# A two-layer trunk on one core: output pieces of the feed-forward stages dealt out in another order

## The chip, the core and the metric

The kernel runs on one core of a Trainium2 chip. A core has engines that run side by side, each with its own queue of instructions worked off in order: TensorE (PE in the profile: matmuls and transposes, with PEld for its weight loads), VectorE (DVE), ScalarE (ACT), GpSimd (POOL, here mostly a source of DMAs) and SyncE (SP, here only DMAs). They meet through semaphores. Matmuls write into PSUM, eight banks of 128 x 512 floats; everything else lives in SBUF. The metric is the device time of one execution in microseconds (us).

## The reference

The input is `x`, 256 tokens of 1024 floats. Two layers follow, each of three steps with a residual and a layer norm:

```
for i in range(2):
    x = LN(alpha * x + 0.5 * swiglu_ffn(x, ffn1_w_in[i], ffn1_w_out[i]))
    x = LN(alpha * x + mixer_i(x))          # 0: sparse attention, 1: state-space scan
    x = LN(alpha * x + 0.5 * swiglu_ffn(x, ffn2_w_in[i], ffn2_w_out[i]))

def swiglu_ffn(x, w_in, w_out):
    gate, up = jnp.split(x @ w_in, 2, axis=-1)      # 1024 -> 2 x 2816
    return (jax.nn.silu(gate) * up) @ w_out         # 2816 -> 1024
```

So there are four feed-forward stages (FFNs), and the change is in them. The mixers stay as they are, except that the scan's last projection ends in the same helper, `tail`.

## The kernel before

**Numbers in two parts.** Every matmul operand is split into a high part (ScalarE casts it, `wh` at L324 for weights, `hH` for activations) and a low remainder (VectorE subtracts, `wl` at L352, `hL`). A product is three matmuls per tile: high by high (L530), one low (L531) and the other low (L532); the helper is `mm3`.

**Weights.** All weights stream through in one long list of units of 128 x 1024 floats, 512 KB. SyncE loads a unit (`raw`, L243), ScalarE makes `wh`, VectorE makes `wl`; a ring of 10 slots holds the pairs. Some units are sums of two loaded ones: VectorE adds them (L291), or GpSimd starts a DMA that adds (L264). `W.pump` makes the next units at given points of the program, so the place of every cast and subtraction in ScalarE's and VectorE's queues is fixed when the program is written. So is everything else: there is no scheduler. Small steps (`later`) are queued by the program and emitted some `step()`s after they were asked for.

**A feed-forward stage.** The inner width 2816 is 22 blocks of 128. `ffn` makes them in three ways:

- *wide*: blocks 0 to 3 as two groups of two. In the first FFN both token halves run side by side; in the other three the first token half (t=0) of both groups comes first, then t=1.
- *seven(j)*: blocks j to j+3 by seven half-size products in place of eight. The products come in the order A11, Q1, piece, Q4, S2, piece, S3, A12, piece, A22, piece; each is 12 matmuls with two units of weights. Two PSUM banks `pmm` (X, Y) and one `ptr` (Z) hold them; ScalarE copies X and Y out (L935, L936, L942, L947), VectorE combines (L919 to L929), and `glu` (L771) does silu on ScalarE (L775) and the multiplication on VectorE (L780). Q1, Q4, S2 and S3 take sums of the activations (`xf`), made by `xT.sums` in eight parts; the others take `xT`.
- *one(j)*: a single block, R below, as two halves, gate and up. Each half is 8 matmuls of 512 columns (L679) and 8 of 256 (L681) into one bank; then ScalarE copies one side out (L887) and VectorE adds the other (L888), which frees the bank. Even blocks use the `pmm` banks, odd ones the `ptr` banks. `turn` (L761) also takes `ptr` banks in turn, for the transposes (L767) of finished activations; ScalarE (L768) and VectorE (L769) split them into `hH` and `hL`.

An *output piece* j multiplies finished activations of block j with 128 rows of the second weight: 12 matmuls into the four `acc` banks, one unit. It can be put anywhere after block j is finished. Pieces thus fill TensorE while other engines prepare the next product. The last six pieces of a stage go to `tail`, which orders them so that the first token half's layer norm can start early: all six pieces of one column half, then all six of the other.

`ffn_steps` deals out the blocks and pieces for all four FFNs alike: S4 with pieces 0, 1, 2, 3; S8 with 6, 7, 4, 5; S12 with 10, 11, 8, 9; S16 with 14, 15, 12, 13; R20; R21; and the tail with 16 to 21. So in all four FFNs the blocks made last (20, 21) are the last two of the tail's list, and the tail follows right behind R21.

Of the kernel before, what the change touches and what calls it, by code (L numbers as in the profile page):

```python
# [21 lines left out]
NJ = FF // 128  # L22
# [38 lines left out]


WIDE = 2
LAG = 6
SEVEN = (4, 8, 12, 16)
MOST = 2500


def ffn_steps():


    steps = []
    for j in SEVEN:
        steps.append(('S', j, [[j - 2], [j - 1], [j - 4], [j - 3]] if j > SEVEN[0] else [[0], [1], [2], [3]]))
    steps += [('R', j, []) for j in range(SEVEN[-1] + 4, NJ)]
    return steps


def ffn_units(ws, wi, wo, wide, lag):
    def colblk(c0):  # L80
        return wi[:, c0:c0 + 128]

    def ktile(blk):
        n = blk.shape[1]
        return blk.reshape(DK, 128, n).transpose(1, 0, 2)

    def out_unit(j):
        ws.append(wo[j * 128:(j + 1) * 128])

    for w in range(wide):  # L90
        j = 2 * w
        blk = np.concatenate([wi[:, j * 128:(j + 2) * 128], wi[:, FF + j * 128:FF + (j + 2) * 128]], axis=1)
        t = ktile(blk)
        for k in range(0, DK, 2):
            ws.append(t[:, k:k + 2].reshape(128, -1))
    def quarter(j, kh):

        blk = np.concatenate([wi[:, j * 128:(j + 2) * 128], wi[:, FF + j * 128:FF + (j + 2) * 128]], axis=1)
        t = ktile(blk)
        return [t[:, k:k + 2].reshape(128, -1) for k in (4 * kh, 4 * kh + 2)]  # L100

    for kind, j, outs in ffn_steps():
        if kind == 'S':
            outs = list(outs)

            def out():
                for o in outs.pop(0):
                    out_unit(o)
# [24 lines left out]


# [57 lines left out]

def all_units(v):
    ws = Plan()
    ffn_units(ws, v['ffn1_w_in'][0], v['ffn1_w_out'][0], WIDE, LAG)
    attn_units(ws, v['attn_w_in'][0], v['attn_w_uk'][0], v['attn_w_uv'][0], v['attn_w_out'][0])
    ffn_units(ws, v['ffn2_w_in'][0], v['ffn2_w_out'][0], WIDE, LAG)
    ffn_units(ws, v['ffn1_w_in'][1], v['ffn1_w_out'][1], WIDE, LAG)
    ssd_units(ws, v['ssm_w_in'][0], v['ssm_w_out'][0])
    ffn_units(ws, v['ffn2_w_in'][1], v['ffn2_w_out'][1], WIDE, LAG)  # L200
    return ws


# [205 lines left out]
def trunk_kernel(ctx: ExitStack, tc: tile.TileContext, widths, forms, x, ln_g, ln_b, wts, kvg, convp,  # L409
                 dt_bias, a_log, d_skip, norm_g, out):  # L410
    nc = tc.nc
# [14 lines left out]
    def f4(s):  # L426
        return wk.tile([128, 1024], F32, name=nm(s), tag="f4", bufs=12)
# [16 lines left out]
    def pmm():  # L444
        return psum.tile([128, 512], F32, name=nm("pmm"), tag="pmm", bufs=2)
# [244 lines left out]
    def tail(acc, c, gb, ks, u, lhs, first, last, hook=None, early=0, ff=False):  # L690

        n = len(ks)
        nxt = None
        m = 0 if last else n - 3
        order = [[(i, hf) for hf in range(2) for i in range(n)],
                 [(i, hf) for i in range(m) for hf in range(2)] + [(i, hf) for hf in range(2) for i in range(m, n)]]
        W.highs(8)
        W.lows()  # L700
        for t in range(2):
            for s, (i, hf) in enumerate(order[t]):
                if s == n and not t and hook:
                    hook()
                if s == n + FILL and t and not last:
                    nxt = XT(ff)
                    nxt.fill(0)
                H, L = W.get(u + i)
                if t and hf and last:
                    continue  # L710
                cs = slice(hf * 512, (hf + 1) * 512)
                mm3(acc[t][hf], *lhs(ks[i], t), H[:, cs], L[:, cs], first and i == 0, i == n - 1)
                if t and hf:
                    W.free(u + i)
                    if s < 2 * n - 2:
                        W.highs()
                        if s < n + FILL - early:
                            W.lows()
            rest = None
            if t and last:  # L720
                rest = pmm()[:, :256]
                for q, ps in enumerate((acc[t][1][:, :256], rest)):
                    ws = slice(512 + q * 256, 768 + q * 256)
                    for i, k in enumerate(ks):
                        H, L = W.get(u + i)
                        mm3(ps, *lhs(k, t), H[:, ws], L[:, ws], q == 1 and i == 0, i == n - 1)
            if t:
                W.lows(len(W.late) - 2)
            layernorm(t, acc[t], c, gb, last, rest, (lambda: W.lows(len(W.late) - 1)) if t and not last else None)
            if not t:  # L730
                W.highs(8)
                W.lows()
        return nxt

    def ffn(xT, u0, ln_i, first=False, last=False, ff=False):
# [3 lines left out]
        u = u0  # L739
# [31 lines left out]
        def glu(t, w, c, sil=None):  # L771


            g, h = (c[:, :256], c[:, 256:]) if sil is None else (sil, f1("h"))
            nc.scalar.activation(g, c[:, :256], AF.Silu)  # L775
            if sil is not None and w >= WIDE:
                nc.scalar.copy(h, c[:, 256:])

            def mul():
                nc.vector.tensor_mul(h, h if w >= WIDE else c[:, 256:], g)  # L780
# [10 lines left out]
        if first:  # L791
# [3 lines left out]
            for w in range(WIDE):  # L795
                ps = [ptr(), ptr()] if w else [pmm(), pmm()]
                for k in range(0, DK, 2):
                    for t in range(2):
                        if (w, k, t) == (0, 0, 1):
                            W.pump(1, now=True)  # L800
                        if (w, k) == (0, 2):
                            xT.fill(t, [1])
                            W.pump(1 + 2 * t, now=True)
                        if (w, k, t) == (0, 4, 1):
                            W.pump(3, now=True)
                        wide(t, w, ps[t], k, k + 2)
# [35 lines left out]
        acc = {}  # L842
# [60 lines left out]
        def seven(j, outs):  # L903


            outs = list(outs)
# [838 lines left out]
```

## Time and profile before

| what | value |
|---|---|
| time, median of 3 runs | 1027.97 us (1027.45 to 1029.94) |
| the profiled execution | 1026.81 us, of which the span of the trace is 1025.0 us |
| busy: PE, DVE, ACT, POOL | 1006.6, 907.9, 660.8, 121.4 us |
| HBM traffic | 193.48 MB read, 190 GB/s over the span |
| first FFN | 0 to 187.65 us |
| sparse attention | 187.65 to 291.14 us |
| second FFN | 291.14 to 469.73 us |
| third FFN | 469.73 to 648.10 us |
| state-space scan | 648.10 to 842.00 us |
| last FFN | 842.00 to 1025.00 us |

How to read it: a row of the timeline gives the start, the length, the engine, the line, what is written and read, and in square brackets how long the engine had stood idle and what released it. One matmul of 512 columns occupies some 0.39 us in these rows, but the next one starts 0.23 us after it; so starts, not lengths, are to be compared on PE. A group row gives the sum of busy time, the mean length in ns, and the idle time before the group with its releasers.

### The profile page before, as it was taken

The numbers are of one execution on the slowest core, as the hardware profiler recorded it, in microseconds if no ns is written. First come the engines' busy times: TensorE is split into PE (matmuls) and PEld (weight loads), VectorE is DVE, ScalarE is ACT, GpSimd is POOL, SyncE is SP. The second block draws the span as 40 slices with busy tenths as digits, with TensorE's granted clock in tenths as the row PEclk, the third lists the DMA queues.
The fourth block names the chain that finished last, engine by engine and source line by source line (L and its number), as shares of the span: only waits on it lengthen the run. The fifth ranks groups of instructions, "written<-read, shape, count | busy, mean of one in ns | idle before, by whom it ended". The sixth has DMA issues, their size and how long they took to land.

```text
span 1025.0 us, 14615 instructions
## 1 busy us (share of the span) xinstructions
PE 1006.6 (98%) x5279; PEld 848.2 (83%) x5279; DVE 907.9 (89%) x1264; ACT 660.8 (64%) x962; POOL 121.4 (12%) x179
## 2 busy tenths in 40 slices
PE   8999999999999999999999999999999999999996
PEld 7788888888787888888778888999899887888885
DVE  6899998789789999988999998788999978999985
ACT  6666776477656667764666775486876645777760
POOL 2101100100011011001101100151111110101101
PEclk9999999999999999999999999999999999999999
DMA  9899999352547899992789999358665654899861
GB/s 332 217 287 276 296 258 360 103 150 98 186 144 171 263 284 295 258 375 78 177 263 281 298 253 348 132 164 249 193 219 187 202 207 108 274 266 254 257 237 41
DMA packets 64664, 231.70 MB, mean 226 GB/s; under 512 B 7280, under 2 KB 7344, under 8 KB 64592
## 3 DMA queue, kind: packets, MB, share of 16 engines
q1 hardware_dynamic: 51264, 183.43, 49.2%
q0 software_dynamic: 13040, 46.82, 23.6%
q8 instruction: 41, 0.67, 0.3%
q10 hardware_dynamic: 288, 0.52, 0.1%
q14 instruction: 31, 0.25, 0.1%
HBM read 193.48 MB, written 1.08 MB: 190 GB/s over the span
## 4 chain that ended last, share of the span: by engine, by line
PE 72%; DVE 14%; DMA 5%; issue 4%; ACT 3%; POOL 1%; POOLq 0%; SPq 0%; DVEq 0%; ACTq 0%
PE pmm L532 10%; PE pmm L530 10%; PE pmm L531 10%; PE acc L530 8%; PE acc L532 8%; PE acc L531 8%; DVE wl L352 7%; DMA raw<-raw 3%; DVE raw L291 2%; DMA raw<-in_wts_dram 2%; ACT wh L324 2%; PE pxs L530 2%; PE pxs L532 2%; PE pxs L531 1%; PE ptr L532 1%
## 5 line engine op out<-in xcount | busy, mean ns | idle before, releaser
L352 DVE TENSOR_TENSOR wl<-raw,wh 128x1024 fp32r<-128x1024 f32 (+2 forms) x423 | 495.0, 1213 | 10.9 <-ACT wh L324 9.9
L324 ACT CAST wh<-raw 128x1024 fp32r<-128x1024 f32 (+3 forms) x430 | 429.6, 1045 | 113.4 <-DVE raw L291 53.7
L530 PE MATMUL acc<-wh,hH 128*128 128x512 f32 (+1 forms) x352 | 138.2, 393 | 0.8 <-ACT hH L893 0.8
L532 PE MATMUL acc<-wh,hL 128*128 128x512 f32 (+1 forms) x352 | 137.1, 390 | 0.9 <-DVE hL L894 0.6
L531 PE MATMUL acc<-wl,hH 128*128 128x512 f32 (+1 forms) x352 | 136.6, 388 | 0.5 <-DVE wl L352 0.5
L530 PE MATMUL pmm<-wh,xT 128*128 128x512 f32 (+2 forms) x320 | 126.4, 395 | 0.0
L532 PE MATMUL pmm<-wh,xT 128*128 128x512 f32 (+2 forms) x320 | 123.9, 387 | 0.1
L531 PE MATMUL pmm<-wl,xT 128*128 128x512 f32 (+2 forms) x320 | 123.3, 385 | 0.0
L264 POOL DMA_DIRECT2D raw<-raw x64 | 55.4, 865 | 449.4 <-DVE raw L291 251.1
L530 PE MATMUL pmm<-wh,xf 128*128 128x512 f32 x256 | 100.4, 392 | 0.9 <-DVE h L780 0.9
L531 PE MATMUL pmm<-wl,xf 128*128 128x512 f32 x256 | 100.1, 391 | 1.1 <-DVE wl L352 1.1
L532 PE MATMUL pmm<-wh,xf 128*128 128x512 f32 x256 | 99.8, 390 | 0.0
L532 PEld LDWEIGHTS acc<-wh,hL 128*128 128x128 f32 x352 | 66.1, 188 | 16.8 <-DVE hL L894 2.2
L530 PEld LDWEIGHTS acc<-wh,hH 128*128 128x128 f32 x352 | 66.1, 188 | 14.4 <-ACT hH L893 1.8
L531 PEld LDWEIGHTS acc<-wl,hH 128*128 128x128 f32 x352 | 66.2, 188 | 13.8 <-DVE wl L352 0.9
L291 DVE TENSOR_TENSOR raw<-raw,raw 128x1024 f32<-128x1024 f32 x64 | 77.0, 1219 | 0.2
L532 PEld LDWEIGHTS pmm<-wh,xT 128*128 128x128 f32 x320 | 60.5, 189 | 13.6 <-DVE xT L527 1.4
L531 PEld LDWEIGHTS pmm<-wl,xT 128*128 128x128 f32 x320 | 60.6, 189 | 11.2 <-DVE wl L352 0.3
L530 PEld LDWEIGHTS pmm<-wh,xT 128*128 128x128 f32 x320 | 60.6, 189 | 10.6
L531 PEld LDWEIGHTS pmm<-wl,xf 128*128 128x128 f32 x256 | 48.1, 188 | 12.1 <-DVE wl L352 2.4
L530 PEld LDWEIGHTS pmm<-wh,xf 128*128 128x128 f32 x256 | 48.0, 188 | 12.0 <-DVE h L780 2.2
L532 PEld LDWEIGHTS pmm<-wh,xf 128*128 128x128 f32 x256 | 48.1, 188 | 10.0
(315 smaller groups left out, 1778.0 us busy)
## 6 DMA issues: line engine op xcount, KB each, us to landing
raw<-in_wts_dram SPq DMA_DIRECT2D x339, 512.0 KB, 6.0
raw<-raw POOLq DMA_DIRECT2D x64, 512.0 KB, 6.1
M<-scr POOLq DMA_DIRECT2D x8, 512.0 KB, 5.7
lng<-in_ln_g_dram POOLq DMA_DIRECT2D x6, 512.0 KB, 5.7
lnb<-in_ln_b_dram POOLq DMA_DIRECT2D x6, 512.0 KB, 6.3
wl<-raw POOLq DMA_DIRECT2D x5, 512.0 KB, 5.5
raw<-in_wts_dram SPq DMA_DIRECT2D x4, 408.0 KB, 7.2
out_dram<-x SPq DMA_DIRECT2D x4, 256.0 KB, 2.1
```

The costliest lines, as they stand in the source:

```text
L264: self.nc.gpsimd.dma_start(self.raw[r], self.raw[other], accum_op=ALU.add)
L291: self.nc.vector.tensor_add(self.raw[r], self.raw[r], self.raw[other])
L324: nc.scalar.copy(h[:, c:c + n], raw[:, c:c + n])
L352: self.nc.vector.tensor_sub(lo[:, s], raw[:, s], h[:, s].bitcast(F32))
L530: nc.tensor.matmul(ps, lh, rh, start=first, stop=False, skip_group_check=on)
L531: nc.tensor.matmul(ps, lh, rl, start=False, stop=False, skip_group_check=on)
L532: nc.tensor.matmul(ps, ll, rh, start=False, stop=last, skip_group_check=on)
```

## The change

The plan of blocks and pieces becomes a function `ffn_plan(first)`, which also names the tail's pieces in order.

- First FFN: R4 and R5 come right behind the wide blocks; then S6 (pieces 0, 1, 2, 3), S10 (4, 5, 8, 9), S14 (6, 7, 12, 13), S18 (10, 11, 16, 17); the tail takes 14, 15, 20, 21, 18, 19.
- Other three: S4 has pieces 0, 1, 2 and none in its last place; S8 has 3, 6, 7, 4; S12 5, 10, 11, 8; S16 9, 14, 15, 12; then R20, R21 and piece 13; the tail takes 16 to 21 as before.
- `tail`: for the first token half both column halves of the first four pieces come first, then both of the last two. In the scan's tail too.
- `seven`: X and Y change places when `j // 4` is odd.
- `glu`: in the three later FFNs ScalarE also copies `h` out of the bank for the last wide group (t=1, w=1); VectorE then multiplies out of SBUF. These are the only added instructions: three on ScalarE.
- `xT.sums`: in the first FFN its eight parts are spread over eight steps rather than four.

```
-        steps.append(('S', j, [[j - 2], [j - 1], [j - 4], [j - 3]] if j > SEVEN[0] else [[0], [1], [2], [3]]))
...
+def ffn_plan(first):
+    if first:
+        s = [(6, [[0], [1], [2], [3]]), (10, [[4], [5], [8], [9]]), (14, [[6], [7], [12], [13]]),
+             (18, [[10], [11], [16], [17]])]
+        return [('R', 4, []), ('R', 5, [])] + [('S', *a) for a in s], [14, 15, 20, 21, 18, 19]
+    s = [(4, [[0], [1], [2], []]), (8, [[3], [6], [7], [4]]), (12, [[5], [10], [11], [8]]),
+         (16, [[9], [14], [15], [12]])]
+    return [('S', *a) for a in s] + [('R', 20, []), ('R', 21, [13])], [16, 17, 18, 19, 20, 21]
...
-        order = [[(i, hf) for hf in range(2) for i in range(n)],
+        order = [[(i, hf) for a, b in ((0, n - 2), (n - 2, n)) for hf in range(2) for i in range(a, b)],
...
-            if sil is not None and w >= WIDE:
+            out_of = sil is not None and (w >= WIDE or (t and w and not first))
+            if out_of:
                 nc.scalar.copy(h, c[:, 256:])
...
-                nc.vector.tensor_mul(h, h if w >= WIDE else c[:, 256:], g)
+                nc.vector.tensor_mul(h, h if out_of else c[:, 256:], g)
...
-                        later(lambda i=i: xT.sums(i), 1 + i // 2)
+                        later(lambda i=i: xT.sums(i), 1 + i)
...
             X, Y, Z = pmm(), pmm(), None
+            if j // 4 % 2:
+                X, Y = Y, X
```

Lines shift: what is L324, L352, L291, L679, L681, L767, L887 and L888 before is L325, L353, L292, L680, L682, L768, L889 and L890 after.

The first place is the start of the first FFN, right behind the wide blocks. On TensorE stood, before, the products of S4; now stand R4 (`pmm` tiles 52 and 57) and R5 (`ptr` tiles 60 and 65), with a transposition into `ptr` tile 63 between. The two `ptr` banks are handed out in turn, so tile 65 lies in the bank of tile 60.

```order
105 L680 MATMUL pmm_52_388<-xT_6_130,wh8_248 128x512 x8
106 L682 MATMUL pmm_52_388<-xT_6_130,wl8_249 128x256 x8
107 L680 MATMUL pmm_57_424<-xT_6_130,wh9_302 128x512 x8
108 L682 MATMUL pmm_57_424<-xT_6_130,wl9_303 128x256 x8
109 L680 MATMUL ptr_60_458<-xT_6_130,wh10_322 128x512 x8
110 L682 MATMUL ptr_60_458<-xT_6_130,wl10_323 128x256 x8
111 L768 MATMUL ptr_63_479<-ident_89,h_45_379 128x128 x2
112 L768 MATMUL ptr_63_479<-ident_89,h_47_382 128x128 x2
113 L680 MATMUL ptr_65_499<-xT_6_130,wh11_352 128x512 x8
114 L682 MATMUL ptr_65_499<-xT_6_130,wl11_353 128x256 x8
115 L531 MATMUL pmm_73_539<-wh12_374,xT_6_130 128x512
```

Four units of weights (8 to 11) now go through TensorE before the first `seven` product, and they are single units, no sums. At the same place ScalarE's queue held, before, casts of units and copies out of the `pmm` banks; `raw` tiles that VectorE has added are read by `wh10`, `wh11`, `wh15` and `wh16` there.

```order
28 L324 CAST wh11_356<-raw_21_197 128x1024
29 L561 CAST xf_42_372<-xq_34_298 128x512
30 L324 CAST wh12_377<-raw_25_228 128x1024
31 L775 ACTIVATE sil_45_383<-ptr_32_282 128x256
32 L775 ACTIVATE sil_47_386<-ptr_33_283 128x256
33 L935 COPY c1_55_395<-pmm_53_393 128x512
34 L936 COPY c2_56_396<-pmm_54_394 128x512
35 L324 CAST wh13_429<-raw_26_254 128x1024
```

And this is ScalarE's queue there now; `wh14` reads `raw_25` and `wh15` reads `raw_26` after VectorE has put a sum into each.

```order
28 L325 CAST wh12_374<-raw_25_228 128x1024
29 L776 ACTIVATE sil_44_378<-ptr_33_284 128x256
30 L776 ACTIVATE sil_46_381<-ptr_34_285 128x256
31 L889 COPY gate_50_386<-pmm_52_388 128x256
32 L562 CAST xf_53_406<-xq_35_300 128x512
33 L325 CAST wh13_416<-raw_26_254 128x1024
34 L325 CAST wh14_420<-raw_25_228 128x1024
35 L889 COPY h_51_387<-pmm_57_424 128x256
36 L900 ACTIVATE gate_50_386<-gate_50_386 128x256
37 L325 CAST wh15_449<-raw_26_254 128x1024
38 L325 CAST wh16_452<-raw_36_306 128x1024
39 L889 COPY gate_58_456<-ptr_60_458 128x256
```

VectorE's queue from the low part of R5's second unit (`wl11`) on reads now:

```order
22 L353 TENSOR_TENSOR wl11_353<-raw_24_226,wh11_352 128x1024
23 L565 TENSOR_TENSOR xf_39_341<-xq_35_300,xf_38_340 128x512
24 L565 TENSOR_TENSOR xf_41_344<-xq_35_300,xf_40_343 128x512
25 L578 TENSOR_TENSOR xq_35_300<-xq_35_300,pxT_11_139 128x512
26 L770 TENSOR_TENSOR hL_8_132<-pht_42_346,hH_7_131 128x512
27 L353 TENSOR_TENSOR wl12_375<-raw_25_228,wh12_374 128x1024
28 L782 TENSOR_TENSOR h_45_379<-ptr_33_284,sil_44_378 128x256
29 L782 TENSOR_TENSOR h_47_382<-ptr_34_285,sil_46_381 128x256
30 L890 TENSOR_TENSOR gate_50_386<-pmm_52_388,gate_50_386 128x256
31 L292 TENSOR_TENSOR raw_25_228<-raw_25_228,raw_27_256 128x1024
```

The last row is the sum that `wh14` reads. On ScalarE, the copy that empties the bank of tile 60 (row 39 there) stands behind the casts `wh15` and `wh16`. On VectorE, the addition that frees the bank (L890 on `gate_58`) stands behind the sum into `raw_26` that `wh15` reads:

```order
34 L890 TENSOR_TENSOR h_51_387<-pmm_57_424,h_51_387 128x256
35 L353 TENSOR_TENSOR wl13_417<-raw_26_254,wh13_416 128x1024
36 L353 TENSOR_TENSOR wl14_421<-raw_25_228,wh14_420 128x1024
37 L292 TENSOR_TENSOR raw_26_254<-raw_26_254,raw_28_258 128x1024
38 L893 TENSOR_TENSOR h_51_387<-h_51_387,gate_50_386 128x256
39 L890 TENSOR_TENSOR gate_58_456<-ptr_60_458,gate_58_456 128x256
```

None of these R steps stood in VectorE's queue at this place before.

The second place is the passage from S4 to S8 in the second FFN (the third and the last have the same order). On ScalarE stood before, with `pmm_425` the bank that holds A22 of S4, and `wh145`, `wh146` both casts of sums by VectorE:

```order
305 L775 ACTIVATE c1_427_3224<-c1_427_3224 128x256
306 L324 CAST wh145_3445<-raw_438_3300 128x1024
307 L775 ACTIVATE sil_448_3463<-pmm_425_3222 128x256
308 L777 COPY h_449_3464<-pmm_425_3222 128x256
309 L324 CAST wh146_3470<-raw_439_3321 128x1024
310 L324 CAST wh147_3473<-raw_442_3370 128x1024
```

And now, with `pmm_426` the bank of A22:

```order
306 L776 ACTIVATE c1_427_3225<-c1_427_3225 128x256
307 L325 CAST wh145_3446<-raw_438_3301 128x1024
308 L776 ACTIVATE sil_447_3462<-pmm_426_3224 128x256
309 L779 COPY h_448_3463<-pmm_426_3224 128x256
310 L325 CAST wh146_3469<-raw_441_3348 128x1024
311 L325 CAST wh147_3472<-raw_442_3371 128x1024
```

The sequence looks the same, but the numbers of the units have moved by one, since the piece behind A22 of S4 has gone: `wh145` was the cast of the first of Q1's two sums and is now the cast of the second. TensorE now has A22, A11 and Q1 one behind the other, and Q1 goes into the bank of A22. VectorE's queue shows the same shift: before, both sums stood together behind `wl144`; now the first stands before `wl143` and the second behind `wl144`.

```order
433 L292 TENSOR_TENSOR raw_437_3299<-raw_437_3299,raw_439_3322 128x1024
434 L782 TENSOR_TENSOR c2_428_3226<-c2_428_3226 128x256
435 L353 TENSOR_TENSOR wl143_3422<-raw_438_3301,wh143_3421 128x1024
436 L353 TENSOR_TENSOR wl144_3426<-raw_437_3299,wh144_3425 128x1024
437 L292 TENSOR_TENSOR raw_438_3301<-raw_438_3301,raw_440_3346 128x1024
438 L782 TENSOR_TENSOR c1_427_3225<-c1_427_3225 128x256
439 L782 TENSOR_TENSOR h_448_3463<-h_448_3463,sil_447_3462 128x256
```

The sum into `raw_438`, which `wh145` reads, is now the second one.

More of the change, by code (lines that the diff above doesn't have):

```diff
@@ L63, with ffn_units @@
 WIDE = 2
-LAG = 6
-SEVEN = (4, 8, 12, 16)
 MOST = 2500
-def ffn_steps():
-    steps = []
-    for j in SEVEN:
-        steps.append(('S', j, [[j - 2], [j - 1], [j - 4], [j - 3]] if j > SEVEN[0] else [[0], [1], [2], [3]]))
-    steps += [('R', j, []) for j in range(SEVEN[-1] + 4, NJ)]
-    return steps
-def ffn_units(ws, wi, wo, wide, lag):
+def ffn_plan(first):
[6 more added lines that the diff above has]
+    return [('S', *a) for a in s] + [('R', 20, []), ('R', 21, [13])], [16, 17, 18, 19, 20, 21]
+def ffn_units(ws, wi, wo, wide, first=False):
     def colblk(c0):
@@ L100, in quarter @@
         return [t[:, k:k + 2].reshape(128, -1) for k in (4 * kh, 4 * kh + 2)]
-    for kind, j, outs in ffn_steps():
+    steps, last = ffn_plan(first)
+    for kind, j, outs in steps:
         if kind == 'S':
@@ L130, in ffn_units @@
                 out_unit(o)
-    for j in range(NJ - lag, NJ):
+    for j in last:
         out_unit(j)
@@ L194, in all_units @@
     ws = Plan()
-    ffn_units(ws, v['ffn1_w_in'][0], v['ffn1_w_out'][0], WIDE, LAG)
+    ffn_units(ws, v['ffn1_w_in'][0], v['ffn1_w_out'][0], WIDE, True)
     attn_units(ws, v['attn_w_in'][0], v['attn_w_uk'][0], v['attn_w_uv'][0], v['attn_w_out'][0])
-    ffn_units(ws, v['ffn2_w_in'][0], v['ffn2_w_out'][0], WIDE, LAG)
-    ffn_units(ws, v['ffn1_w_in'][1], v['ffn1_w_out'][1], WIDE, LAG)
+    ffn_units(ws, v['ffn2_w_in'][0], v['ffn2_w_out'][0], WIDE)
+    ffn_units(ws, v['ffn1_w_in'][1], v['ffn1_w_out'][1], WIDE)
     ssd_units(ws, v['ssm_w_in'][0], v['ssm_w_out'][0])
-    ffn_units(ws, v['ffn2_w_in'][1], v['ffn2_w_out'][1], WIDE, LAG)
+    ffn_units(ws, v['ffn2_w_in'][1], v['ffn2_w_out'][1], WIDE)
     return ws
@@ L958, in seven @@
             out()
-        for kind, j, outs in ffn_steps():
+        steps, ks = ffn_plan(first)
+        for kind, j, outs in steps:
             W.raws = 9 if j < 18 else 7
@@ L969, in ffn @@
         gb = load_ln(ln_i)
-        return u + LAG, tail(acc, 0.5, gb, list(range(NJ - LAG, NJ)), u, lhs, False, last, ff=ff)
+        return u + len(ks), tail(acc, 0.5, gb, ks, u, lhs, False, last, ff=ff)
     def attention(xT, u, ln_i):
```

## The prediction

> **What bounds the kernel now.** I read the busy times of the page first, then the groups of TensorE's matmuls with what they waited for, then timelines at the three kinds of place that the change touches.
>
> ```profile
> PE 1006.6 (98%) x5279; PEld 848.2 (83%) x5279; DVE 907.9 (89%) x1264; ACT 660.8 (64%) x962; POOL 121.4 (12%) x179
> L530 PE MATMUL acc<-wh,hH 128*128 128x512 f32 (+1 forms) x352 | 138.2, 393 | 0.8 <-ACT hH L893 0.8
> L530 PE MATMUL pmm<-wh,xf 128*128 128x512 f32 x256 | 100.4, 392 | 0.9 <-DVE h L780 0.9
> ```
>
> TensorE is the bound: 98% of the span, and its groups stood idle about a microsecond each. It is idle 1025.0 - 1006.6 = 18.4 us in all. So a new wait of TensorE cannot be made good later, and what the change can gain is what these few waits hold. VectorE is second, at 89%; where TensorE waits, it is for VectorE or for ScalarE behind it. The change moves no matmul out of the program. I therefore count waits of TensorE that go and waits that come.
>
> **Waits that go, first.** At the start of the first FFN, S4's first piece and its Q4 wait for their low weights.
>
> ```profile
> 37.54 0.39 PE L530 MATMUL acc<-wh,hH 128*128 128x512 f32 x1
> 38.40 0.50 PE L531 MATMUL acc<-wl,hH 128*128 128x512 f32 x1 [0.47 <-DVE wl L352]
> ...
> 41.03 0.39 PE L530 MATMUL pmm<-wh,xf 128*128 128x512 f32 x1
> 42.47 0.50 PE L531 MATMUL pmm<-wl,xf 128*128 128x512 f32 x1 [1.05 <-DVE wl L352]
> ```
>
> Undisturbed matmuls start 0.23 us apart (twelve of them from 340.79 to 343.51, in rows further down). So these two lose 0.86 - 0.23 = 0.63 and 1.44 - 0.23 = 1.21 us. R4 and R5 need no sums and give VectorE time, so both go: -1.85 us.
>
> Then the tail. Blocks 20 and 21 are finished only just before it, and its fifth and sixth matmul groups wait for their activations.
>
> ```profile
> 172.29 0.39 PE L531 MATMUL acc<-wl,hH 128*128 128x512 f32 x1
> 172.92 0.50 PE L532 MATMUL acc<-wh,hL 128*128 128x512 f32 x1 [0.24 <-DVE hL L894]
> 173.69 0.50 PE L530 MATMUL acc<-wh,hH 128*128 128x512 f32 x1 [0.27 <-ACT hH L893]
> 454.27 0.39 PE L531 MATMUL acc<-wl,hH 128*128 128x512 f32 x1
> 454.98 0.50 PE L532 MATMUL acc<-wh,hL 128*128 128x512 f32 x1 [0.33 <-DVE hL L894]
> 455.75 0.50 PE L530 MATMUL acc<-wh,hH 128*128 128x512 f32 x1 [0.27 <-ACT hH L893]
> ```
>
> In the first FFN that is (0.63 - 0.23) + (0.77 - 0.23) = 0.94 us, in the second 0.48 + 0.54 = 1.02. The group row gives 0.8 us of such waits for `hH` in all, three of 0.27, so the third FFN has one, worth 0.54 like the others, and the last none. With piece 13 (2.72 us) behind R21, and four pieces ahead of the two fresh ones, all go: -2.5 us. Next in line is the layer norm of the first token half: VectorE adds the first column half (L613) and takes its statistics (L624).
>
> ```profile
> 176.62 0.69 DVE L624 BATCH_NORM_STATS2 st<-x 128x6 f32<-128x512 f32 x1
> 178.79 0.69 DVE L613 SCALAR_TENSOR_TENSOR x<-acc,x 128x512 f32<-128x512 f32 x1 [1.48 <-PE acc L532]
> ```
>
> The pair takes 0.68 + 0.69, about 1.4 us, and VectorE was done with it 1.48 us ahead of the second half. Now the first column half ends only two groups of three matmuls, 6 x 0.23 = 1.4 us, ahead of the second. That is just covered; I charge 0.1 us for each of the four tails, +0.4, between nothing and 0.8.
>
> Third, Q1 of S4 waits in the three later FFNs for VectorE to multiply out of the bank; the group row on `h` L780 shows 0.9 us for the three. ScalarE's new copy empties the bank instead.
>
> ```profile
> 317.53 0.38 ACT L775 ACTIVATE sil<-pmm 128x256 f32<-128x256 f32 x1
> 317.94 0.42 DVE L780 TENSOR_TENSOR h<-pmm,sil 128x256 f32<-128x256 f32 x1
> 318.42 0.50 PE L530 MATMUL pmm<-wh,xf 128*128 128x512 f32 x1 [0.30 <-DVE h L780]
> ```
>
> The silu itself starts at 317.53, behind casts; it gives way after some 0.3 us (0.38 in its row, less the overlap) and I take as much for a copy of the same 256 columns, with 0.05 between, so the bank would be free at 318.2, against 317.94 + 0.42 = 318.36 by VectorE. So 0.17 us goes, not the whole wait: -0.5 us for three. If ScalarE's copy only came in level, nothing.
>
> **A wait that comes: R5.** The order puts the second half of R5 into the `ptr` bank that its first half used. That bank is free once ScalarE has copied one side and VectorE added the other; both stand behind sums and casts in their queues. The trace of before has the durations:
>
> ```profile
> 28.91 0.60 PE L767 MATMUL pht<-ident,h 128*128 128x128 f32 x4
> 32.10 0.39 PE L530 MATMUL pmm<-wh,xT 128*128 128x512 f32 x1
> ...
> 993.35 2.00 PE L679 MATMUL ptr<-xT,wh 128*128 128x512 f32 x8
> 996.14 2.00 PE L679 MATMUL ptr<-xT,wh 128*128 128x512 f32 x8
> ...
> 38.28 5.99 ACT L324 CAST wh<-raw 128x1024 fp32r<-128x1024 f32 x6
> ...
> 31.12 0.69 DVE L564 TENSOR_TENSOR xf<-xq,xf 128x512 fp32r<-128x512 f32 x1
> 41.20 6.89 DVE L352 TENSOR_TENSOR wl<-raw,wh 128x1024 fp32r<-128x1024 f32 x6
> ```
>
> TensorE reaches the wide blocks' end at 32.10 in both programs. A half of R takes 996.14 - 993.35 = 2.79 us, a turn of four transposes some 0.36 (the 0.60 of its row, less what the next matmul overlaps), so R5's second half could start at 32.10 + 3 x 2.79 + 0.36 = 40.8.
>
> VectorE gets there later. One 1024-wide operation costs 6.89 / 6, near 1.14 us; a 512-wide one 0.61 (0.69 in the row, less the overlap with its neighbour); a 256-wide one 0.33 likewise (0.42 in the row above). The transposes at 28.91 give `hH` to ScalarE, whose cast ends near 30.1; `wh11` follows (1.0 us a cast, 5.99 / 6), and `wl11` can start at 31.1. From there VectorE has, in its new order (shown with the change): `wl11` 1.14, four of 512 columns 2.44, `wl12` 1.14, three of 256 columns 1.0, a sum 1.14: 38.0. Now `wh14`, which reads that sum, runs until 39.0, and the copy of `h_51` behind it until 39.4. VectorE adds (0.33), makes `wl13` and `wl14` and the sum for `wh15` (3 x 1.14): 43.2. Casts `wh15`, `wh16` and the copy of `gate_58` take 2.4 us more: 45.6. VectorE's addition frees the bank at 46.0.
>
> 46.0 - 40.8 = 5.2 us of wait. Behind it the weights for S6 are ready, so nothing is late next; and nothing absorbs it. From below, if VectorE skipped the wait for `wh14`'s copy (1.4 us), it is 3.8; from above, each DMA that lands late in this first part can add a microsecond: 6.5. I take +5.2.
>
> A stop of 5 us also touches the clock.
>
> ```profile
> 1012.00:1016.00 4.00, 3.67 (x31) 3.47 (x29) 2.97 (x7) 0.00 (x0) 0.00 (x0) 1.00 0.35 131
> 1016.00:1020.00 4.00, 0.00 (x0) 0.00 (x0) 3.45 (x7) 0.00 (x0) 1.69 (x2) 1.00 0.00 0
> 1021.00:1025.00 4.00, 0.00 (x0) 0.00 (x0) 0.00 (x0) 0.00 (x0) 0.00 (x0) 0.50 0.20 75
> ```
>
> After the last matmul (about 1015.7, from 3.67 us busy in the first row) the granted clock, the third figure from the end, stood at 1.00 for 4 us of idleness and at 0.50 from 1021 on. So it fell some 5 us after the last matmul, and a wait of 5.2 us is near that. I count no drop in the sum. [...]
>
> **A wait that comes three times: S4 to S8.** In the three later FFNs no piece stands behind A22 of S4, so TensorE goes A22, A11, Q1, and Q1 needs A22's bank.
>
> ```profile
> 340.79 0.39 PE L530 MATMUL pmm<-wh,xT 128*128 128x512 f32 x1
> 343.51 0.39 PE L530 MATMUL acc<-wh,hH 128*128 128x512 f32 x1
> 358.42 0.39 PE L530 MATMUL pmm<-wh,xf 128*128 128x512 f32 x1
> ...
> 340.26 0.68 DVE L929 TENSOR_TENSOR c<-ptr,c 128x512 f32<-128x512 f32 x1
> ...
> 345.91 1.05 ACT L324 CAST wh<-raw 128x1024 fp32r<-128x1024 f32 x1 [4.51 <-DVE raw L291]
> 346.87 0.37 ACT L775 ACTIVATE sil<-pmm 128x256 f32<-128x256 f32 x1
> ```
>
> A22 starts at 340.79, a product lasts 2.72 us, so Q1 could start at 340.79 + 5.44 = 346.2. Before, ScalarE emptied A22's bank behind a cast that waited 4.51 us for the first of two sums; the piece then covered it. Now that cast reads the second sum. VectorE from 340.26: L929 0.61, `wl` 1.14, sum 1.14, 0.33, two `wl` 2.28, sum 1.14: 346.9. Cast, silu and copy (1.05, 0.37 and, by the silu, 0.3) take 1.7 more: 348.6. So TensorE waits 2.4 us. Q1 then runs to 351.4, transposes 0.36; the piece behind it needs a `wl` that VectorE ends at 352.4 (multiplication 0.33, `wl`, sum, `wl`, from 348.6), 0.5 us late. Adding Q4's two transposes 0.36 and Q4, S2 starts at 358.1, against 358.42 before. But by then before had done one piece more, 2.72 us, which stands behind R21 now, where TensorE is as full as anywhere. Loss: 2.72 - 0.3 = 2.4 us.
>
> The chain hangs on VectorE's clock alone, S2 at the start of L929 plus 17.8 us, so I carry it to the other two.
>
> ```profile
> 519.15 0.68 DVE L929 TENSOR_TENSOR c<-ptr,c 128x512 f32<-128x512 f32 x1
> 887.78 0.68 DVE L929 TENSOR_TENSOR c<-ptr,c 128x512 f32<-128x512 f32 x1
> 537.32 0.39 PE L530 MATMUL pmm<-wh,xf 128*128 128x512 f32 x1
> 906.05 0.39 PE L530 MATMUL pmm<-wh,xf 128*128 128x512 f32 x1
> ```
>
> S2 comes at 537.0 and 905.6: losses 2.72 - 0.37 and 2.72 - 0.45. Together +7.0 us. From below: were the sums made a whole 1.14 us sooner, 1.3 each, +3.8; from above, no gain at S2 at all, 8.2.
>
> **At nothing.** X and Y change places, but the pool deals the banks out the other way since ScalarE empties the last wide bank; the two cancel, and X stands in the same bank as before. The activation sums in eight steps are used from Q1 of S6 on, which now comes at about 51.5 (46.0 + 2.79 + 2.72) and came at 34.8 (32.10 + 2.72). The layer norm's parameters are now loaded behind S18 in the first FFN; the tail's first half runs 36 matmuls, 8.2 us, before they are read, and before the same load stood the same way behind R21. The adding DMAs move with their blocks.
>
> **The sum.** +7.0 + 5.2 - 1.85 - 2.5 - 0.5 + 0.4 = +7.75 us. On the profiled execution (1026.81 us, 1.8 around its span of 1025.0) that is 1034.6. It lies 1.16 us under the median of the runs, 1027.97; on that median the sum gives 1035.7, which I state.
>
> **The rivals.**
>
> - *VectorE and ScalarE run ahead (faster).* The two new waits rest on VectorE's queue. If VectorE had the second sum 2.4 us sooner and R5's addition 5.2 us sooner, only the gains would be left: -4.85 + 0.4 = -4.4, 1023.5 us. For it: ScalarE is busy only 64%, and at S4 to S8 it idles 4.51 us. Against: the bracket of that row names VectorE as the releaser, so it is VectorE's queue that would have to be shorter, and its length is counted above. Chance 0.09.
> - *Only one of the two waits comes.* Without R5's: +2.55, 1030.5. Without S8's: +0.75, 1028.7. The two places share no instruction; each could be misread by itself. 0.13.
> - *Sums sooner at S8*, by the lower bound above: 1.14 x 3 less, 1032.3. 0.1.
> - *The clock falls in R5's wait.* At the start matmuls stood 0.43 us apart instead of 0.23 (8.25 to 8.68 below); seven such matmuls, 3 us, cost 7 x 0.2 = 1.4 us: 1037.1, and 1038.5 if it stays slow for twice as long. [...] 0.13.
>
> ```profile
> 8.25 0.63 PE L532 MATMUL pmm<-wh,xT 128*128 128x512 f32 x1
> 8.68 0.63 PE L530 MATMUL pmm<-wh,xT 128*128 128x512 f32 x1
> ```
>
> **How the numbers follow.** The forecast itself, both waits at about these sizes, has 0.55. A measurement can tell 0.3%, 3.1 us, from no change: under 1024.9 is faster, over 1031.1 slower. Faster: the first rival, 0.09. Same: the second, 0.13. Slower: 0.55 + 0.1 + 0.13 = 0.78. The range goes from R5's wait alone (1028.7, with a little room 1028.5) to the slow clock's far end (1038.5). It holds the bounds of the two waits, 3.8 + 3.8 (1031.1) and 6.5 + 8.2 (1038.2), and leaves out the first rival and a slow clock on top of the upper bounds.
>
> **What would show it.** In the changed profile: the first L680 row into `ptr` after 40.8 with an idle time near 5 us behind VectorE's L890; the first `xf` product of S8 idle near 2.4 us behind ScalarE's `h` copy in each later FFN, and no `hH` L895 waits in the tails. Wrong would be: R5's second half starting by 42, or Q1 of S8 right behind A11. If both are there and the time is still near 1028, then TensorE had slack that I didn't see.

## The result, and the profile after

The changed kernel takes 1042.25 us (median of 4 runs, 1040.13 to 1044.8) against 1028.19 (1027.45 to 1029.94) before: a ratio of 1.0135, 95% interval 1.0109 to 1.0162, or 14 us more. The forecast was slower by 7.75 us, at 1035.7 with a range up to 1038.5. So the sign was right and the size was not; the time lies outside the range.

The profiled execution took 1040.13 us, with a span of 1038.4. First the page's busy times and its row of the granted clock in 40 slices (a 9 is 90% or more).

```profile
span 1038.4 us, 14640 instructions
PE 1011.4 (97%) x5279; PEld 853.5 (82%) x5279; DVE 908.4 (87%) x1264; ACT 661.2 (64%) x965; POOL 121.6 (12%) x179
PEclk9899999999999999999999999999999999999998
```

The same 5279 matmuls and transposes keep TensorE busy 1011.4 us in place of 1006.6: 4.8 us of the loss, net, are not idleness at all, but longer matmuls. The rest, 13.4 - 4.8 = 8.6 us, is idleness. The second slice of the clock, 26 to 52 us, is an 8.

TensorE's groups with their idle time name the first cause. One row has changed from 0.9 to 7.6 us; the waits of the `acc` groups for `hH`, `hL` and `wl` are gone.

```profile
L531 PE MATMUL acc<-wh,hH 128*128 128x512 f32 (+1 forms) x352 | 137.9, 392 | 0.0
L533 PE MATMUL acc<-wh,hL 128*128 128x512 f32 (+1 forms) x352 | 136.7, 388 | 0.0
L532 PE MATMUL acc<-wl,hH 128*128 128x512 f32 (+1 forms) x352 | 136.4, 387 | 0.0
L531 PE MATMUL pmm<-wh,xf 128*128 128x512 f32 x256 | 103.0, 402 | 7.6 <-ACT h L779 7.2
```

TensorE's timeline at the two kinds of place, R5 first, then Q1 of S8 in the second, third and last FFN:

```profile
39.73 0.60 PE L768 MATMUL ptr<-ident,h 128*128 128x128 f32 x4
45.28 3.78 PE L680 MATMUL ptr<-xT,wh 128*128 128x512 f32 x8 [4.96 <-DVE gate L890]
48.86 1.63 PE L682 MATMUL ptr<-xT,wl 128*128 128x256 f32 x8
50.33 0.39 PE L531 MATMUL pmm<-wh,xT 128*128 128x512 f32 x1
...
353.15 0.50 PE L531 MATMUL pmm<-wh,xf 128*128 128x512 f32 x1 [2.50 <-ACT h L779]
...
533.97 0.50 PE L531 MATMUL pmm<-wh,xf 128*128 128x512 f32 x1 [2.47 <-ACT h L779]
...
905.95 0.50 PE L531 MATMUL pmm<-wh,xf 128*128 128x512 f32 x1 [2.24 <-ACT h L779]
```

All four stops are where the prediction put them, with the releasers it named and nearly its sizes (5.2 and 2.4). But R5's second half takes 50.33 - 45.28 = 5.05 us after its stop, where a half took 2.79. The stretches of the trace around the first two stops tell why; the third figure from the end is the granted clock.

```profile
40.00:45.00 5.00, 0.33 (x3) 0.09 (x1) 3.01 (x5) 2.49 (x4) 0.88 (x1) 0.82 0.52 99
45.00:47.00 2.00, 1.72 (x4) 1.43 (x5) 2.00 (x3) 2.00 (x4) 0.00 (x0) 0.50 1.04 197
47.00:49.00 2.00, 2.00 (x6) 1.52 (x6) 2.00 (x3) 0.66 (x1) 0.00 (x0) 0.50 0.25 37
49.00:51.00 2.00, 2.00 (x12) 1.90 (x11) 1.98 (x4) 0.41 (x2) 0.00 (x0) 0.74 0.58 229
...
350.00:353.00 3.00, 0.65 (x3) 0.19 (x1) 1.76 (x3) 1.49 (x4) 0.86 (x1) 1.00 0.76 143
353.00:354.00 1.00, 0.85 (x3) 0.72 (x4) 0.87 (x2) 1.00 (x3) 0.00 (x0) 0.91 0.68 131
354.00:357.00 3.00, 3.00 (x8) 2.30 (x7) 3.00 (x4) 1.48 (x3) 0.00 (x0) 0.50 0.70 131
357.00:358.00 1.00, 1.00 (x8) 0.82 (x6) 1.00 (x1) 0.00 (x0) 0.00 (x0) 0.89 0.19 12
```

The clock is at half its rate (0.50 in these rows) behind every one of the stops (the other two are taken up below). At S8 it falls only after the stop is over: a mean of 0.91 from 353 to 354 puts the fall at 353.82 (0.18 us at half rate), and TensorE had been back since 353.15.

The stages, by the first transposition of the next stage's `x` on TensorE in both traces:

| stage | before | after | difference |
|---|---|---|---|
| first FFN, start to 184.04 and 187.72 | 184.04 | 187.72 | +3.68 |
| attention, to 287.50 and 291.50 | 103.46 | 103.78 | +0.32 |
| second FFN, to 466.12 and 473.20 | 178.62 | 181.70 | +3.08 |
| third FFN, to 644.56 and 654.02 | 178.44 | 180.82 | +2.38 |
| scan, to 835.85 and 845.30 | 191.29 | 191.28 | 0.0 |
| last FFN, to the end of the span | 189.15 | 193.10 | +3.95 |

The four FFNs, with the tail's end that falls into the attention row, hold the whole difference of the two spans.

### The profile page after: what moved, and what is told of

The parts are those of the page before. It is cut to its first block, busy times and chain, and to the rows that moved or that the text cites. A ratio compares the mean times of both kernels' runs of the same rounds, so it can differ in the third digit from the quotient of the medians.

```text
span 1038.4 us, 14640 instructions
## 1 busy us (share of the span) xinstructions
PE 1011.4 (97%) x5279; PEld 853.5 (82%) x5279; DVE 908.4 (87%) x1264; ACT 661.2 (64%) x965; POOL 121.6 (12%) x179
## 4 chain that ended last, share of the span: by engine, by line
PE 68%; DVE 14%; issue 7%; DMA 6%; ACT 3%; POOL 1%; POOLq 0%; DVEq 0%; ACTq 0%
PE pmm L531 9%; PE pmm L533 9%; PE pmm L532 9%; PE acc L531 7%; PE acc L533 7%; PE acc L532 7%; DVE wl L353 6%; DMA raw<-raw 5%; DVE raw L292 2%; ACT wh L325 2%; PE pxs L531 1%; PE pxs L533 1%; PE pxs L532 1%; PE ptr L680 1%; PE ptr L531 1%
## 5 line engine op out<-in xcount | busy, mean ns | idle before, releaser
L353 DVE TENSOR_TENSOR wl<-raw,wh 128x1024 fp32r<-128x1024 f32 (+2 forms) x423 | 495.9, 1213 | 13.5 <-ACT wh L325 12.5
L325 ACT CAST wh<-raw 128x1024 fp32r<-128x1024 f32 (+3 forms) x430 | 430.1, 1045 | 112.4 <-DVE raw L292 60.3
L531 PE MATMUL pmm<-wh,xf 128*128 128x512 f32 x256 | 103.0, 402 | 7.6 <-ACT h L779 7.2
L533 PE MATMUL pmm<-wh,xf 128*128 128x512 f32 x256 | 101.5, 396 | 0.0
L292 DVE TENSOR_TENSOR raw<-raw,raw 128x1024 f32<-128x1024 f32 x64 | 77.2, 1219 | 0.3
L531 PEld LDWEIGHTS pmm<-wh,xf 128*128 128x128 f32 x256 | 49.0, 191 | 20.1 <-ACT h L779 10.1
L533 PEld LDWEIGHTS pmm<-wh,xf 128*128 128x128 f32 x256 | 49.3, 192 | 10.7
```

The source lines that it names most:

```text
L292: self.nc.vector.tensor_add(self.raw[r], self.raw[r], self.raw[other])
L325: nc.scalar.copy(h[:, c:c + n], raw[:, c:c + n])
L353: self.nc.vector.tensor_sub(lo[:, s], raw[:, s], h[:, s].bitcast(F32))
L531: nc.tensor.matmul(ps, lh, rh, start=first, stop=False, skip_group_check=on)
L533: nc.tensor.matmul(ps, ll, rh, start=False, stop=last, skip_group_check=on)
```

## The experiments

Theory A, formed on this trace: the sum was right about the waits, and what lacked is the clock, which falls in or behind each of the four stops and stays down for some 3.4 us of work or more. Rivals: the slow matmuls only fill time in which TensorE would have waited for VectorE (B), or the loss lies elsewhere (C). Beside busy_stops, later_before, both_before and one_unit the kernel before measured 1028.2 us (16 runs), beside the other four 1028.56 (13 runs); all ratios are to these.

**busy_stops: work that needs nothing, put into the stops.**

```
+        def busy(pool, n):
+            b = [pool(), pool()][0]
+            for i in range(n):
+                nc.tensor.transpose(b[:, (i % 4) * 128:(i % 4 + 1) * 128], ident, ident)
...
+                if first and j == 5 and o is h:
+                    busy(pmm, 44)
...
+            if not first and j == 8:
+                busy(ptr, 20)
```

> The kernel after with transposes of the identity put into the four stops of TensorE: 44 of them ahead of R5's second half in the first FFN, 20 between A11 and Q1 of S8 in each later FFN. They write a free PSUM bank that nothing reads; no wait is taken away. Theory A (each stop also halves the granted clock for about 3.4 us of work behind it): the stops keep their length, but the clock stays at 1.00 and 2.3 us at R5 and 1.3 to 1.8 us at each S8 come back, together about 7 us: 1033 us in the profile, about 1035 in the median of runs, which is where the hand sum lay. Theory B (the slow matmuls only fill time in which TensorE would have waited for VectorE anyway): no change, 1042 us. Theory C (the extra time is not at these places): no change, and the clock stays low.

Measured: 1035.29 us (1034.29 to 1035.91), ratio 1.0069 (1.0054 to 1.0085). TensorE's timeline at R5, and the stretches at S8 of the second FFN:

```profile
39.33 0.60 PE L768 MATMUL ptr<-ident,h 128*128 128x128 f32 x4
39.76 4.97 PE L877 MATMUL pmm<-ident 128*128 128x128 f32 x44
44.88 2.11 PE L680 MATMUL ptr<-xT,wh 128*128 128x512 f32 x8
46.83 1.11 PE L682 MATMUL ptr<-xT,wl 128*128 128x256 f32 x8
47.78 0.40 PE L531 MATMUL pmm<-wh,xT 128*128 128x512 f32 x1
```

```profile
347.00:350.00 3.00, 3.00 (x23) 2.71 (x22) 2.32 (x3) 0.93 (x1) 0.48 (x1) 1.00 0.92 175
350.00:353.00 3.00, 2.90 (x16) 2.22 (x15) 2.30 (x3) 3.00 (x6) 0.38 (x1) 1.00 0.79 149
353.00:354.00 1.00, 1.00 (x9) 0.82 (x7) 1.00 (x2) 0.05 (x1) 0.00 (x0) 1.00 0.49 90
354.00:357.00 3.00, 2.84 (x14) 2.11 (x13) 3.00 (x4) 2.38 (x4) 0.00 (x0) 1.00 0.54 171
```

R5's second half starts 5.55 us after the turn, as in after (45.28 - 39.73; here 44.88 - 39.33, the turn's row standing ahead of the transposes), but lasts 47.78 - 44.88 = 2.90 us, and the clock is at 1.00 throughout; its mean over the whole run is 0.998, as before the change, in place of 0.989. The kernel does more work and is 7 us faster. That is theory A; B and C fall. The time is 0.4 us from the 1035.7 that the hand sum gave without a clock term. That it comes so close is partly luck: the runs themselves spread over 1.6 us.

**later_before: the three later FFNs as before.**

```
-    s = [(4, [[0], [1], [2], []]), (8, [[3], [6], [7], [4]]), (12, [[5], [10], [11], [8]]),
-         (16, [[9], [14], [15], [12]])]
-    return [('S', *a) for a in s] + [('R', 20, []), ('R', 21, [13])], [16, 17, 18, 19, 20, 21]
+    s = [(4, [[0], [1], [2], [3]]), (8, [[6], [7], [4], [5]]), (12, [[10], [11], [8], [9]]),
+         (16, [[14], [15], [12], [13]])]
+    return [('S', *a) for a in s] + [('R', 20, []), ('R', 21, [])], [16, 17, 18, 19, 20, 21]
```

> The kernel after, but the three later FFNs have the pieces of before (S4 with 0, 1, 2, 3 and so on, none behind R21). The first FFN, the tail's order, ScalarE's copy and the swap stay as in after. Theory A: S8's stop and its slow clock go from all three, 9.4 us by the stage boundaries, and the tails' gains (1.0, 0.5, 0) and Q1's 0.17 each stay: 1042.2 - 9.4 - 1.8 = 1031.0 us. Rival (piece 13 behind R21 is what spares the tail its waits, not the tail's order): the waits come back, 1032.6 us. Rival (TensorE only moves its stop to another place of these stages): about 1040.

Measured: 1030.5 us (1028.7 to 1032.21, 11 runs), ratio 1.002 (1.0011 to 1.0028). The three stops go, and the tails have no waits for `hH` either, though piece 13 no longer stands behind R21:

```profile
L531 PE MATMUL acc<-wh,hH 128*128 128x512 f32 (+1 forms) x352 | 137.9, 392 | 0.0
L533 PE MATMUL acc<-wh,hL 128*128 128x512 f32 (+1 forms) x352 | 136.9, 389 | 0.9 <-DVE hL L770 0.9
...
L531 PE MATMUL pmm<-wh,xf 128*128 128x512 f32 x256 | 100.3, 392 | 0.4
```

The 0.9 us are three waits for the `hL` that `turn` makes, at 358.08, 536.10 and 905.09, in pieces of S8 and not in a tail. So the tail's order spares the waits, not the moved piece, and the pieces' new places in the later FFNs bring nothing that was not to be had without them.

**both_before: all pieces and blocks as before.** The edit of later_before, the old plan for the first FFN too, and the activation sums in four steps; of the change the tail's order, ScalarE's copy and the swap are left.

```
-    if first:
+    if False:
...
-                        later(lambda i=i: xT.sums(i), 1 + i)
+                        later(lambda i=i: xT.sums(i), 1 + i // 2)
```

> The pieces and blocks of before in all four FFNs, and the activation sums in four steps as before; of the change only the tail's order, ScalarE's extra copy and the swap stay. Theory A: all four stops go, and what the tail's order (-2.5 + 0.4) and the copy (-0.5) gain stays: 1028.2 - 2.6 = 1025.6 us, faster than before. Rival (these three edits gain nothing by themselves): 1028.2.

Measured: 1025.37 us (1024.3 to 1026.67, 6 runs), ratio 0.9972 (0.9961 to 0.9984). Faster than before, as theory A has it.

**tail_only: before, with the new order of the tail alone.**

```
-        order = [[(i, hf) for hf in range(2) for i in range(n)],
+        order = [[(i, hf) for a, b in ((0, n - 2), (n - 2, n)) for hf in range(2) for i in range(a, b)],
```

> The kernel before with the new order of the tail's pieces alone (first token half: both column halves of the first four pieces, then of the last two). Theory A (the tail's waits for the fresh activations are the gain, as summed: -2.5 + 0.4): 1028.2 - 2.1 = 1026.1 us, and the timeline of the tails shows no wait for hH or hL. Rival (the gain of both_before came from ScalarE's extra copy and the swap): 1028.2 us.

Measured: 1024.75 us (1024.14 to 1027.92, 9 runs), ratio 0.9965 (0.9954 to 0.9977). TensorE's groups:

```profile
L530 PE MATMUL acc<-wh,hH 128*128 128x512 f32 (+1 forms) x352 | 137.8, 392 | 0.0
L532 PE MATMUL acc<-wh,hL 128*128 128x512 f32 (+1 forms) x352 | 136.8, 389 | 0.6 <-DVE hL L769 0.6
...
L530 PE MATMUL pmm<-wh,xf 128*128 128x512 f32 x256 | 100.4, 392 | 0.9 <-DVE h L780 0.9
```

The tail's waits (for `hH` L893 and `hL` L894, 0.8 and 0.6 us before) are gone. The 0.6 us that the row still shows are two waits for an `hL` made by `turn` (L769), at 353.54 and 531.15, ahead of the tails. Q1's waits for `h` stay, since the copy is not in this kernel. This single line is the whole gain that can be measured: it cannot be told from both_before.

**one_unit: fewer weights made behind R4 and R5.**

```
+            n = 1 if first else 2
             later(half(g))
-            step(most=None)
+            step(n, most=None)
...
             later(mul, 2)
-            step(most=None)
+            step(n, most=None)
```

> The kernel after, but behind each half of R4 and R5 in the first FFN one unit of weights is made instead of two, so that ScalarE's copy and VectorE's addition that free the bank no longer stand behind two casts and a sum. Theory A: R5's second half waits some 1.9 us instead of 5.1, too short for the clock to fall; 3.2 + 2.3 us come back: 1036.7 us. Rival (VectorE is short of time there in any order, so the wait moves on to Q1 of S6 or its first piece): the stop at R5 shrinks, one of the same length comes some 5 us later, 1042.

Measured: 1037.28 us (1034.22 to 1037.85), ratio 1.0081 (1.0064 to 1.0097). TensorE at R5:

```profile
40.09 0.60 PE L768 MATMUL ptr<-ident,h 128*128 128x128 f32 x4
42.39 2.11 PE L680 MATMUL ptr<-xT,wh 128*128 128x512 f32 x8 [1.71 <-DVE gate L890]
44.35 1.11 PE L682 MATMUL ptr<-xT,wl 128*128 128x256 f32 x8
45.30 0.40 PE L531 MATMUL pmm<-wh,xT 128*128 128x512 f32 x1
```

A stop of 1.7 us instead of 5, no slow matmuls behind it (2.91 us for the half), and no new wait of more than 0.25 us up to the attention. So R5's stop came from ScalarE's and VectorE's queues, not from a lack of time on VectorE. The S8 of the second FFN got worse: A11 waits 0.79 us for a low weight and Q1 2.52 us for the bank, and the clock stays down for 6.83 us, from 347.68 to 354.51, where it was 3.4 in after. One of the four runs was spared some of that: it took 1034.22 us at a mean clock of 0.994, the others 1037.19 to 1037.85 at 0.991.

**s8_queue: ScalarE empties A22's bank ahead of the cast that waits.** In S4 of the later FFNs the step of the third piece comes behind A22.

```
-            out()
+            out_pieces(outs.pop(0), outs[-1])
             product(X, "A22", False)
             glu(1, w, X, f1("sil"))
+            if not outs[-1]:
+                step()
             step()
...
-                step()
+                if then:
+                    step()
```

> The kernel after, but in the three later FFNs the casts that were queued behind the third piece of S4 are queued behind A22 instead, so that ScalarE's silu and copy that empty A22's bank stand ahead of the cast that waits for the second sum. Theory A (the bank only names the wait; VectorE's chain of sums and subtractions is what sets it): Q1 of S8 no longer waits for the bank, but A11 waits some 1.2 us for a low weight and Q1 twice some 0.9; S2 comes no earlier, perhaps 0.7 us later; since no single stop is over 1.3 us the clock holds and 1.3 to 1.8 us each come back: about 1038 us. Rival (ScalarE's order is the cause): the whole loss of S8 goes, 2.4 + 1.6 us three times, 1030 us.

Measured: 1039.26 us (1038.0 to 1040.66), ratio 1.0101 (1.0083 to 1.0119). The rows of TensorE's timeline at S8 that have a bracket, and the stretches there:

```profile
352.81 0.50 PE L532 MATMUL pmm<-wl,xT 128*128 128x512 f32 x1 [1.61 <-DVE wl L353]
356.21 0.50 PE L531 MATMUL pmm<-wh,xf 128*128 128x512 f32 x1 [0.61 <-ACT wh L325]
357.47 0.50 PE L532 MATMUL pmm<-wl,xf 128*128 128x512 f32 x1 [0.76 <-DVE wl L353]
```

```profile
350.00:353.00 3.00, 1.39 (x7) 0.85 (x6) 1.81 (x3) 1.47 (x4) 0.85 (x1) 1.00 0.69 158
353.00:356.00 3.00, 2.60 (x11) 1.79 (x10) 2.36 (x3) 0.89 (x1) 0.45 (x1) 1.00 0.35 66
356.00:359.00 3.00, 2.03 (x9) 1.43 (x10) 2.81 (x3) 2.42 (x4) 0.41 (x1) 1.00 0.75 143
```

The wait for the bank is gone and three waits for weights stand in its place, 2.98 us in all, more than the 2.50 of after; the releaser that the profile had named (ScalarE's copy) was only the last of a chain. By the medians the kernel is 3.0 us faster than after, though the intervals of the two ratios overlap. TensorE stands idle longer (29.9 us of the span in place of 27.0) and is busy for less (1008.8 in place of 1011.4), so what is gained is the clock: it stays at 1.00 at all three S8, where the idleness lies in three pieces, the longest of 1.61, 1.40 and 1.23 us at the three places, and falls only at R5. ScalarE's order as the cause falls.

**no_stop: the first FFN's new plan without the queue in front of R5.** later_before, and:

```
+            n = 1 if first and j == 4 else 2
             later(half(g))
-            step(most=None)
+            step(n, most=None)
...
             later(mul, 2)
-            step(most=None)
+            if first and j == 4:
+                items()
+            else:
+                step(n, most=None)
```

> The pieces of before in the three later FFNs; the first FFN's new plan, but no weights are made behind R4's second half and only one unit behind its first, so that the addition that frees the bank for R5's second half stands right behind R4's. Theory A: R5's second half starts within 0.2 us of its turn, a wait of some 0.5 us for a low weight comes at Q1 of S6; against both_before (1025.4) the 1.85 us of waits at the start go: 1024.1 us, and the clock stays up. Rival (VectorE is short of time there in any order): the same 1.9 us as with one unit, at Q1 or the first piece of S6: 1025.4 us.

Measured: 1024.49 us (1024.1 to 1025.64, 5 runs), ratio 0.9959 (0.9945 to 0.9974).

```profile
40.96 2.14 PE L680 MATMUL ptr<-xT,wh 128*128 128x512 f32 x8 [0.54 <-DVE gate L890]
...
50.37 0.50 PE L532 MATMUL acc<-wl,hH 128*128 128x512 f32 x1 [0.64 <-DVE wl L353]
```

R5's stop is down to 0.54 us, and a wait of 0.64 came at S6's first piece, not at Q1. The first FFN's tail waits 0.75 us for an `hL` at 171.01, which both_before and tail_only, with the old plan, do not show. It is the fastest kernel here by its median, but its interval overlaps those of tail_only and both_before: whether R4 and R5 at the start are worth anything once their stop is gone stays open.

**busy_half: half of the transposes.** busy_stops with `busy(pmm, 22)` and `busy(ptr, 10)`.

> As busy_stops, but with half the transposes, first in each stop: 22 ahead of R5's second half, 10 ahead of Q1 of S8. TensorE then idles about 2.7 us at R5 and 1.5 us at each S8 in one piece. Theory A1 (the clock falls where idleness fills most of a stretch of 3.4 us, as in the stops of 2.5 us of after): it holds at the three S8 and falls at R5 as it did at S8 of after: 1035.3 + 1.5 to 2.3 = 1037.2 us. Theory A2 (any stop over a microsecond brings it down): 1040 or more. Theory A3 (2.7 us is too little by itself): 1035.3.

Measured: 1036.14 us (1035.66 to 1036.29), ratio 1.0069 (1.0055 to 1.0084). TensorE idled 2.57 us at R5, and the clock stayed up:

```profile
41.14 2.57 PE L877 MATMUL pmm<-ident 128*128 128x128 f32 x22
46.27 0.96 PE L680 MATMUL ptr<-xT,wh 128*128 128x512 f32 x3 [2.57 <-DVE gate L897]
```

```profile
43.00:46.00 3.00, 0.70 (x7) 0.46 (x5) 1.01 (x3) 2.50 (x4) 0.88 (x1) 1.00 0.23 44
46.00:49.00 3.00, 2.73 (x15) 2.39 (x16) 3.00 (x4) 2.66 (x4) 0.00 (x0) 1.00 0.74 139
```

Against its own kernel before the ratio is that of busy_stops, 1.0069, so A3 held and A1's fall at R5 did not come. So the length of a stop alone does not tell whether the clock falls: it held through 2.57 us here and fell behind 2.24 us in the last FFN of after. Why it held is not shown.

## Why the prediction failed, point by point

- **R5's wait, +5.2:** 4.96 us idle in the trace of after, and 45.28 - 39.73 - 0.36 = 5.19 by the starts, as the working counted it; right, with its chain.
- **S4 to S8, +7.0:** stops of 2.50, 2.47 and 2.24 us where 2.4 was said; right. That VectorE's chain sets it and not the bank was part of the working, and s8_queue shows it. The low weight that was to be late by 0.5 us behind Q1 shows only with the clock up (0.16 us idle in busy_stops, 354.59 - 353.95 - 0.23 = 0.41 by the starts); in after the slow matmuls cover it.
- **Waits that go, -1.85 and -2.5:** gone in after. With R5's stop filled or gone a wait for an `hL` comes back in the first FFN's tail (0.76 us in busy_stops at 174.02, 0.75 in no_stop), so "all go" was too much for the first FFN. The tail's part is shown by tail_only, -2.1 with the layer norm's charge; it measured 3.8 us (interval 2.4 to 4.7 by the ratio), so the sum was, if anything, low. By the stages of its trace the first three FFNs are shorter by 0.28, 0.82 and 0.85 us, 1.95 together, near the sum; where the rest of the medians' gain lies the trace doesn't show.
- **Q1 of S4, -0.5:** from 322.21 - 321.70 and its two likes, the excess is 0.28 us in place of 0.46; about the 0.17 each that was said.
- **The swap at nothing:** X and Y take the same banks with and without the swapping line, as the built program shows; the reason I gave (ScalarE's copy) was not tested by itself.
- **"I count no drop in the sum": this step failed.** It rested on the end of the trace of before, where the clock stayed up for over 4 us after the last matmul (it ended at 1015.67; a mean of 0.96 from 1020 to 1021 puts the fall at 1020.92, 5.25 us later), and read that as a length which a stop must reach. I weighed a fall only at R5, at 1.4 us and a chance of 0.13 (seven slow matmuls, as many as the trace of before has at its start, from 7.25 to 10.38), and for S8, with stops half as long, not at all. It fell at all four. R5's second half cost 5.05 - 2.79 = 2.3 us more. At each S8 seven matmuls stood 0.43 us apart and one on either side was slowed in part: in the second FFN nine steps from start to start, from 353.72 to 357.36, took 3.64 us where nine of 0.227 take 2.04, so 1.6 us. Together 2.3 + 3 x 1.6 = 7.1; busy_stops got 7.0 back by medians. The forecast with this term, 7.75 + 7.1 = 14.85, is 0.8 above the 14.06 measured. The profiled execution of after lost 0.7 us less to slow matmuls at its start (last section), which is nearly that much; whether the other three executions did so too is not known.

How long the clock stayed down can be read off the windows of after.

```profile
43.00:44.00 1.00, 0.00 (x0) 0.00 (x0) 0.00 (x0) 1.00 (x2) 0.88 (x1) 0.60 0.00 0
...
50.00:50.50 0.50, 0.50 (x5) 0.50 (x5) 0.50 (x2) 0.00 (x0) 0.00 (x0) 0.97 0.47 189
...
534.00:535.00 1.00, 1.00 (x4) 0.81 (x5) 1.00 (x2) 1.00 (x2) 0.00 (x0) 0.86 0.99 193
...
538.00:539.00 1.00, 1.00 (x8) 0.86 (x7) 1.00 (x2) 0.00 (x0) 0.00 (x0) 0.93 0.36 57
...
906.00:907.00 1.00, 1.00 (x4) 0.87 (x5) 1.00 (x2) 1.00 (x2) 0.00 (x0) 0.89 1.01 197
...
910.00:911.00 1.00, 1.00 (x7) 0.81 (x7) 1.00 (x2) 0.00 (x0) 0.00 (x0) 0.91 0.27 49
```

At S8 of the second FFN it fell at 353.82 and was back at 357.22 (0.89 from 357 to 358): 3.40 us. In the third and the last FFN the rows above put it down from 534.72 to 538.14 and from 906.78 to 910.18: 3.42 and 3.40. At R5 the mean of 0.60 puts the fall at 43.2 and the 0.97 the return at 50.03: 6.8 us.

What brings it down is open. It fell in or behind single stops of 4.96, 2.50, 2.47 and 2.24 us in after; it held at R5 through the 1.71 us of one_unit and the 2.57 of busy_half, and at S8 of the second FFN through the 2.98 us that s8_queue has in three waits. The end of the traces gives no length either: in before the fall came 5.25 us after the last matmul, in after 3.96 (that one ended at 1029.10, and a mean of 0.53 from 1033 to 1034 puts the fall at 1033.06). So the 5 us there were no length that a stop has to reach.

## What to carry to other kernels

Where a change makes TensorE wait, price the wait and the clock behind it: a stop of 2.2 to 2.5 us cost here another 1.6, and one of 5 us another 2.3. At R5 the clock held through a single stop of 1.71 us in one_unit and through one of 2.57 in busy_half; a length up to which a stop is safe is not shown. Three short waits of 3 us together were, by the medians, cheaper than one of 2.5, and transposes whose result nobody reads, put into the four stops, gave 7 us back. A releaser that the profile names can be only the last link, as at S8; ask what it waited for before moving it.

## What the runs showed of the hardware

The clock fell behind a stop as well as in one: at S8 of the second FFN TensorE had worked for 0.67 us (from 353.15 to 353.82) when it was halved, at R5 it fell at 43.2, 2.1 us ahead of the stop's end at 45.28. At the kernel's start the last matmul that followed its neighbour at the slow spacing of 0.43 us began at 10.38 us in before and at 9.04 in after. The first of these matmuls starts at 7.25 in before and 7.18 in after, the one behind the next four transposes at 12.00 and 11.26: 0.74 - 0.07 = 0.67 us, which made up some of R5's loss. (The clock's column reads 1.00 in these first microseconds; only the spacing shows it.) The runs of one kernel differ in the clock: of the 11 of later_before, the three with a mean clock of 0.996 took 1028.7 to 1029.14 us, the eight with 0.994 or 0.995 took 1030.16 to 1032.21. That it was a stretch at half clock that these three were spared is argued, not shown, since only one execution of each kernel has a trace. The spread of after (1040.13 to 1044.8) against that of busy_stops (1034.29 to 1035.91) may have the same source; that stays open.
